# A two-layer hybrid decoder in fp32 parts: order of the first weights, place of the first norm's column and sums, and the last scale cut in parts

## The chip, the cores and the metric

The kernel runs on one core of a Trainium2 chip. The metric is device time in microseconds of one execution, as the median of several runs. The engines are called PE (TensorE, with PEld for its weight loads), DVE (VectorE), ACT (ScalarE), POOL (GpSimd) and SP (SyncE, which here only issues transfers). A name with q behind it (SPq, ACTq) is that engine's queue of instructions where it issues a DMA.

## The reference

A trunk of two layers over 256 tokens of width 1024. Each layer is a half-step SwiGLU (width 2816), attention, and a second half-step SwiGLU, each behind an RMS norm of the stream; a last RMS norm ends the trunk. Everything is float32.

```python
def rmsnorm(x, g):
    y = x * rsqrt(mean(x * x, axis=-1, keepdims=True) + RMS_EPS)
    return y * g

def swiglu(h, w_gate, w_up, w_down):
    return (silu(h @ w_gate) * (h @ w_up)) @ w_down

for layer in range(2):
    h = h + 0.5 * swiglu(rmsnorm(h, ffn1_norm[layer]), ...)
    hn = rmsnorm(h, mix_norm[layer])
    h = h + (mixer_a(hn, ...) if layer == 0 else mixer_b(hn, ..., shared))
    h = h + 0.5 * swiglu(rmsnorm(h, ffn2_norm[layer]), ...)
    if layer == 0:
        shared = shared_kv(h, kv_norm, kv_w, pos)
return rmsnorm(h, final_norm)
```

`mixer_a` is a causal dilated sliding-window attention with 16 heads of 64, `mixer_b` a block-sparse attention over shared keys and values. The change touches neither: it touches the first `swiglu` and the last `rmsnorm`.

## The kernel before

**Number format.** Each weight comes from memory as float32 (`raw`), and is cut in two parts in TensorE's reduced float format: ACT makes the high part `wh` by a copy (line 167, in the opening line 182), DVE the low part `wl` as the difference (line 168, in the opening line 183). Activations are cut in the same way. A product is then wh by (xh, xl), 512 columns wide (line 204), plus wl by xh, 256 wide (line 210). Where such a product adds in one PSUM bank, the first half of the bank and the second have to be summed at the end: `joined` (ACT copies one half at line 341, DVE adds the other at line 342).

**The feed-forward blocks.** `ffn_blocks` runs over the hidden width in 22 groups of 128 columns, f = 0 to 21. Weights come in units of two groups: one transfer of 1 MB for gate (g) and one for up (u), each split in two halves. Their order on SP's queue is the order of the calls. The pool of raw tiles has 4 buffers, that of wh and wl 8 each. Accumulators come from a pool of 5 PSUM banks (`accp`) and another of 3 (`trp`); a group needs one for gate and one for up. `close` sums and scales a finished group, and makes of it the operand of the down projection. It runs after the products of the next group have been issued.

**The opening.** For f = 0 and 1 of the first feed-forward block the weights come in five pieces over the contraction blocks k (`OPENING`: k = 0, k = 1, then two at a time), so that products can begin as soon as k = 0 is there. The x block of a piece (`first`, line 822; the first one carries the gains too) is transferred and scaled by the norm's gain (ACT line 99, DVE line 97) ahead of the piece's split. The gate weights of the first three pieces are issued on ACT's queue (line 113), everything else on SP's queue. Eight products of PE on a constant tile (line 119) run meanwhile.

**The norm.** The products use x times its gain only; the factor 1/rms belongs to the token and is put on the finished group. `Norm.square` sums the squares of the blocks (ACT line 245, DVE line 246 for the first norm). `Norm.finish` makes the column of 1/rms: a product on PE (line 251), its reader on DVE (line 253), a power on POOL (line 255). `Norm.spread` makes a row of it, the same on all partitions: two diagonal matrices on DVE (line 262), two products on PE (line 263), a copy on DVE (line 265). `close` multiplies by that row (line 372 on DVE, line 375 on POOL), so `spread` runs ahead of the first `close`. For the first block `finish` is called by `products_t` between the first products of gate and up at f = 2.

**The end.** `down_last` closes the four quarters of the last down projection (two token tiles t, two column halves c). Each close is followed by DVE's sum into h (line 590; line 595 for the last 256 columns), ACT's sum of squares (line 886; DVE line 882 for the last 256) and DVE's product with the final gain (line 890). `total` and the power (lines 894 and 902) run on POOL. `finish` then scales the 1024 columns of the token tile, half on ACT (line 903) and half on DVE (line 904), and sends the two halves (line 906).

**Order on an engine.** A scheduler orders the instructions of each engine from the order in the code and its own model of durations; `issue_after`, used through `queued` and `marks`, holds an instruction back in that order until a named one has been placed. Each engine then works through its list strictly in order.

Of the kernel before, what the change touches and what calls it, by code (L numbers as in the profile page):

```python
# [10 lines left out]
F32 = mybir.dt.float32  # L11
F32R = mybir.dt.float32r
AF = mybir.ActivationFunctionType
ALU = mybir.AluOpType

P = 128
S = 256
NT = S // P
D = 1024
KD = D // P  # L20
# [15 lines left out]
         ("ffn1_norm", 1), ("mix_norm", 1), ("ffn2_norm", 1)]  # L36

LAST_O = ("o", H // 2 - 1)
OPENING = ((0, 1), (1, 1), (2, 2), (4, 2), (6, 2))
GX = len(GAINS) * KD  # L40

# [26 lines left out]
def trunk(ctx: ExitStack, tc: tile.TileContext, a: dict, out: bass.AP):  # L68
    nc = tc.nc
    PS = bass.MemoryType.PSUM  # L70
    const = ctx.enter_context(tc.tile_pool(name="const", bufs=1))
    rawp = ctx.enter_context(tc.tile_pool(name="rawp", bufs=4))
# [35 lines left out]

    both = const.tile([P, GX + KD * S], F32, name="gains_hT")
    gT, hT = both[:, :GX], both[:, GX:].rearrange("p (k s) -> p k s", s=S)  # L110
    early = {k: rawp.tile([P, 2, n, S], F32, tag="raw", name=f"raw_0_{k}") for k, n in OPENING[:3]}
    for k, n in OPENING[:3]:
        nc.scalar.dma_start(early[k][:, 0], a["ffn1_w_gate"][0][k * P:(k + n) * P, :S].rearrange("(k p) n -> p k n", p=P))
    BF16 = mybir.dt.bfloat16
    fill = const.tile([P, 512], BF16, name="fill")
    nc.vector.memset(fill, 1.0)
# [37 lines left out]
    def unit(name, k, n, srcs, behind=()):  # L154

        raw = rawp.tile([P, k, n], F32, tag="raw", name=f"raw_{name}")
        for dst, src in srcs:
            nc.sync.dma_start(raw if dst is None else raw[:, :, dst], src)
        pieces = []
        behind = iter(behind)  # L160
        for j in range(0, k, 1024 // n):
            kk = min(1024 // n, k - j)
            wh = wp.tile([P, kk, n], F32R, tag="wh", name=f"wh_{name}_{j}")
            wl = wp.tile([P, kk, n], F32R, tag="wl", name=f"wl_{name}_{j}")
            r = raw[:, j:j + kk, :]
            with queued(next(behind, None)):
                nc.scalar.activation(wh, r, AF.Copy)  # L167
                nc.vector.tensor_sub(wl, r, wh.bitcast(F32))  # L168
            for i in range(kk):
                pieces.append((wh[:, i, :], wl[:, i, :]))  # L170
        return pieces

    def opening(wg, wu, before):


        for k, n in OPENING:
            raw = early.get(k) or rawp.tile([P, 2, n, S], F32, tag="raw", name=f"raw_0_{k}")
            wh, wl = [wp.tile([P, 2, n, S], F32R, tag=tag, name=f"{tag}_0_{k}") for tag in ("wh", "wl")]
            before(k, n)
            for i, w in list(enumerate((wg, wu)))[k in early:]:  # L180
                nc.sync.dma_start(raw[:, i], rows(w, k, n, 0, S))
            marks["opening"] = [nc.scalar.activation(wh, raw, AF.Copy)]
            nc.vector.tensor_sub(wl, raw, wh.bitcast(F32))
            for j in range(n):
                yield [(wh[:, i, j, :], wl[:, i, j, :]) for i in range(2)]

    def rows(w, k0, k, c0, n):
        return w[k0 * P:(k0 + k) * P, c0:c0 + n].rearrange("(k p) n -> p k n", p=P)
# [10 lines left out]
    def products_t(acs, wss, xs, first, last, between=None):  # L199


        for ac, ws in zip(acs, wss):
            for i, ((wh, wl), x) in enumerate(zip(ws, xs)):
                nc.tensor.matmul(ac, wh, flat(x), start=first and i == 0, stop=False)  # L204
            if between is not None:
                between()
                between = None
        for ac, ws in zip(acs, wss):
            for i, ((wh, wl), x) in enumerate(zip(ws, xs)):
                nc.tensor.matmul(ac[:, :S], wl, x[:, 0, :], start=False, stop=last and i == len(ws) - 1)  # L210
# [127 lines left out]
    def joined(ac, name):  # L338

        s = etile(f"j_{name}")  # L340
        nc.scalar.activation(s, ac[:, S:], AF.Copy)  # L341
        nc.vector.tensor_add(s, ac[:, :S], s)  # L342
        return s
# [13 lines left out]
    def ffn_blocks(name, wg, wu, norm, first=None, beside=(), sums=None, queue=()):  # L357

        blocks, pairs, rest = [], {}, []

        def both(f, pair):
            acs = [acc(f"{name}_{n}{f}") for n in "gu"]
            cols = slice(f % 2 * P, (f % 2 + 1) * P)
            products_t(acs, [[(wh[:, cols], wl[:, cols]) for wh, wl in w] for w in pair], norm.x, True, True,
                       norm.finish if norm.col is None else None)
            return acs

        def close(f, gate, up):  # L370
            g = joined(gate, f"{name}_g{f}")
            nc.vector.tensor_mul(g, g, norm.row)  # L372
            nc.scalar.activation(g, g, AF.Silu)  # L373
            u = joined(up, f"{name}_u{f}")
            nc.gpsimd.tensor_tensor(u, u, norm.row, op=ALU.mult)  # L375
            pair = f // 2
            if sums is not None and pair in sums:
                if f % 2 == 0:
                    pairs[pair] = atile([P, 2, S], name=f"act2_{name}_{f}")
                prod = pairs[pair][:, f % 2]  # L380
            else:
                prod = g
            nc.vector.tensor_mul(prod, g, u)  # L383
            x = atile([P, 2, S], F32R, name=f"act_{name}_{f}")
            parts_of(x[:, 0], x[:, 1], prod)
            while rest:
                rest.pop(0)()
            if prod is not g and f % 2:
                rest.extend(quarter_sums(pairs.pop(pair), *sums[pair], f"{name}_{f}"))
            blocks.append(x)  # L390

        done = []

        def close_all():
            if done and norm.row is None:
                norm.spread()
            for args in done:
                close(*args)
            done.clear()

        for f in range(0, KF, 2):
            if f == 0 and first is not None:
                ws = opening(wg, wu, first)
            else:
                ws = zip(*[unit(f"{name}_{n}{f}", KD, S, [(None, rows(w, 0, KD, f * P, S))], queue[2 * f + j:2 * f + j + 2])
                           for n, w, j in (("g", wg, 0), ("u", wu, 2))])
            if f == 0:
                acs = [[(trt if i and n == "u" else acc)(f"{name}_{n}{i}") for n in "gu"] for i in range(2)]
                for k, pair in enumerate(ws):
                    for i in range(2):  # L410
                        for ac, (wh, wl) in zip(acs[i], pair):
                            cols = slice(i * P, (i + 1) * P)
                            products_t([ac], [[(wh[:, cols], wl[:, cols])]], norm.x[k:k + 1], k == 0, k == KD - 1)
                    while norm.late:
                        norm.late.pop(0)()
                if first is not None:
                    with queued("opening"):
                        for k in range(KD):
                            norm.square(k)
                elif norm.col is None:  # L420
                    norm.finish()
                done += [(i, *acs[i]) for i in range(2)]
                continue
            pair = list(zip(*ws))
            for call in beside[f // 2 - 1:f // 2]:
                call()
            for i in (f, f + 1):
                acs = both(i, pair)
                close_all()
                done.append((i, *acs))  # L430
        close_all()
        return blocks

# [14 lines left out]
    def ffn(name, layer, which, norm, after, first=None, beside=(), homes=("kx4", "kx6", "qkh", "qkh"), queue=()):  # L448
        wg, wu, wd = (a[f"ffn{which}_w_{n}"][layer] for n in ("gate", "up", "down"))
        sums = left_sums(homes)  # L450
        blocks = ffn_blocks(name, wg, wu, norm, first, beside, sums, queue)
        if which == 1:
            table(AF.Exp, blocks[-1][:, 0, 0:1].bitcast(F32))
        down(f"{name}_d", wd, blocks, sums, after)
# [371 lines left out]
    n0, n1, n2 = Norm(0, "n0", nc.vector), Norm(1, "n1"), Norm(2, "n2")  # L826
    n3, n5, n6 = Norm(4, "n3"), Norm(5, "n5"), Norm(6, "n6")

    ffn("f10", 0, 1, n0, n1, first)
    late_constants()  # L830
    xs = n1.xs()
    w, n = a["a_w_qkv"][0], HG * DH
# [66 lines left out]
    def finish(t):  # L899
        v = total(t) if len(parts[t]) > 1 else parts[t][0]  # L900
        r = sp.tile([P, 1], F32, tag="rmsf", name=f"rms_{t}")
        nc.gpsimd.tensor_tensor(r, v, expo, op=ALU.pow)
        nc.scalar.activation(outs[t][0], outs[t][0], AF.Copy, scale=r)
        nc.vector.tensor_scalar_mul(outs[t][1], outs[t][1], r)
        for c in range(2):
            (nc.scalar, nc.sync)[c].dma_start(out[0, t * P:(t + 1) * P, c * 512:(c + 1) * 512], outs[t][c])

    down_last("f21_d", a["ffn2_w_down"][1], blocks, sums, h, 0.5, finish_part, finish)

# [26 lines left out]
```

## Time and profile before

| | us |
|---|---|
| median of the 3 runs | 979.35 |
| lowest and highest of them | 978.72, 980.27 |
| profiled execution | 978.82 |
| its span, first to last instruction | 977.0 |
| busy: PE, PEld, DVE, ACT, POOL | 966.6, 832.2, 813.9, 612.2, 286.0 |

A row of the order of time has the start in us, the duration in us (from the first start to the last end where it stands for several), the engine, the line, the operation with what it writes and reads, the shapes, the count, and in brackets how long the engine was idle before it and what ended that. A row of the chain of waits has the start, the duration, and the engine and line that the end of the span hung on for that time; "issue" is time in which the engine waited for nothing that the profile shows. Names in rows are those of the tiles without their numbers: `raw` is a piece of the opening, `raw_f_g` and `raw_f_u` are units of gate and up, `gains_hT` the x blocks. Ends of matrix products are modelled, since they are pipelined.

### The profile page before, as it was taken

How to read it: one execution, taken by the hardware profiler on the slowest of the kernel's cores; microseconds unless marked ns; L12 is line 12 of the kernel's file. 1: busy time of each engine (PE TensorE's matmuls, PEld its weight loads, DVE VectorE, ACT ScalarE, POOL GpSimd, SP SyncE). 2: the span in 40 equal slices, each digit the busy share in tenths (PEclk: the TensorE clock that was granted, in tenths of full speed). 3: DMA queues.
4: the chain of work that ended last, by engine and by line, in shares of the span. 5: the costliest groups of instructions: out<-in, count | busy, mean ns of one | idle time of the engine just before them, and what ended most of it. 6: DMA issues, size and time to landing. Idle time of an engine off the chain costs nothing.

```text
span 977.0 us, 14859 instructions
## 1 busy us (share of the span) xinstructions
PE 966.6 (99%) x5391; PEld 832.2 (85%) x5391; DVE 813.9 (83%) x1390; ACT 612.2 (63%) x1131; POOL 286.0 (29%) x235
## 2 busy tenths in 40 slices
PE   9999999999999999999999999999999999999997
PEld 6888888878889888888888888888888998888886
DVE  7988899887878788889898888987787878888995
ACT  7756656566777665656576655656577766666561
POOL 0211246143432211146032121612143322112461
PEclk9999999999999999999999999999999999999999
DMA  9876536664334656545755565483734345665351
GB/s 314 285 218 202 185 129 229 206 212 163 122 104 148 189 181 195 184 158 199 256 172 174 173 181 208 169 278 114 256 127 133 108 154 171 186 201 175 130 172 43
DMA packets 126858, 176.00 MB, mean 180 GB/s; under 512 B 3393, under 2 KB 106305, under 8 KB 126785
## 3 DMA queue, kind: packets, MB, share of 16 engines
q1 hardware_dynamic: 125936, 174.01, 54.9%
q10 hardware_dynamic: 848, 1.05, 0.3%
q8 instruction: 42, 0.69, 0.3%
q14 instruction: 32, 0.25, 0.1%
HBM read 173.99 MB, written 1.05 MB: 179 GB/s over the span
## 4 chain that ended last, share of the span: by engine, by line
PE 93%; DVE 2%; DMA 2%; ACT 2%; issue 1%; POOL 0%; SPq 0%; POOLq 0%; ACTq 0%; DVEq 0%
PE f_g L204 16%; PE f_u L204 16%; PE f_u L210 8%; PE f_g L210 8%; PE dn_f_d L197 6%; PE dn_f_d L193 6%; PE dn_f_d L195 6%; PE dn_f_d_m L197 1%; PE dn_f_d_m L193 1%; PE dn_f_d_m L195 1%; PE qk_a L193 1%; PE qk_a L197 1%; PE qk_a L195 1%; DMA raw_f_u<-in_ffn_w_up_dram 1%; PE v_a L193 1%; PE q_b L193 1%
## 5 line engine op out<-in xcount | busy, mean ns | idle before, releaser
L375 POOL TENSOR_TENSOR j_f_u<-j_f_u,r_n 128x256 f32<-128x256 f32 x88 | 93.7, 1067 | 355.9 <-DVE j_f_u L342 339.6
L204 PE MATMUL f_g<-x_n,wh_f_g 128*128 128x512 f32 x688 | 180.4, 394 | 1.0 <-DVE j_f_g L342 1.0
L204 PE MATMUL f_u<-x_n,wh_f_u 128*128 128x512 f32 x688 | 177.3, 390 | 0.0
L204 PEld LDWEIGHTS f_u<-x_n,wh_f_u 128*128 128x128 f32 x688 | 129.1, 188 | 27.3
L204 PEld LDWEIGHTS f_g<-x_n,wh_f_g 128*128 128x128 f32 x688 | 124.0, 189 | 23.9 <-DVE j_f_g L342 1.2
L168 DVE TENSOR_TENSOR wl_f_u<-raw_f_u,wh_f_u 128x1024 fp32r<-128x1024 f32 x86 | 113.0, 1317 | 1.0 <-ACT wh_f_u L167 1.0
L168 DVE TENSOR_TENSOR wl_f_g<-raw_f_g,wh_f_g 128x1024 fp32r<-128x1024 f32 x86 | 104.9, 1236 | 0.8 <-ACT wh_f_g L167 0.7
L210 PE MATMUL f_u<-x_n,wl_f_u 128*128 128x256 f32 x688 | 103.3, 283 | 0.0
L210 PE MATMUL f_g<-x_n,wl_f_g 128*128 128x256 f32 x688 | 102.9, 282 | 0.0
L210 PEld LDWEIGHTS f_g<-x_n,wl_f_g 128*128 128x128 f32 x688 | 96.4, 190 | 6.3
L167 ACT ACTIVATE wh_f_u<-raw_f_u 128x1024 fp32r<-128x1024 f32 x86 | 88.0, 1048 | 11.8 <-PE f_g L204 7.5
L167 ACT ACTIVATE wh_f_g<-raw_f_g 128x1024 fp32r<-128x1024 f32 x86 | 89.4, 1048 | 5.1 <-PE f_g L204 2.7
L373 ACT ACTIVATE j_f_g<-j_f_g 128x256 f32<-128x256 f32 x88 | 36.7, 417 | 88.5 <-DVE j_f_g L372 88.2
L210 PEld LDWEIGHTS f_u<-x_n,wl_f_u 128*128 128x128 f32 x688 | 91.6, 192 | 0.0
L246 POOL TENSOR_TENSOR ss_n<-ss_n,sq_n 128x256 f32<-128x256 f32 x35 | 32.2, 921 | 141.2 <-ACT sq_n L245 139.4
L99 ACT ACTIVATE act_f<-j_f_g 128x256 fp32r<-128x256 f32 x58 | 24.0, 418 | 55.3 <-DVE j_f_g L383 55.3
L383 DVE TENSOR_TENSOR j_f_g<-j_f_g,j_f_u 128x256 f32<-128x256 f32 x58 | 27.4, 477 | 29.9 <-POOL j_f_u L375 29.9
L492 POOL TENSOR_TENSOR sum_f_d_6b<-sum_f_d_6ac,raw_f_d 128x512 f32<-128x512 f32 x4 | 44.4, 11092 | 17.6 <-DVE sum_f_d_6ac L491 13.2
L342 DVE TENSOR_TENSOR j_f_g<-f_g,j_f_g 128x256 f32<-128x256 f32 x88 | 36.6, 416 | 11.8 <-ACT j_f_g L341 11.8
L685 POOL TENSOR_SCALAR sm_a<-sm_a,ls_a 128x128 f32<-128x128 f32 (+1 forms) x32 | 30.4, 964 | 47.8 <-DVE ls_a L683 42.1
L685 POOL TENSOR_SCALAR sm_b<-sm_b,ls_b 128x128 f32<-128x128 f32 (+1 forms) x32 | 29.0, 924 | 49.9 <-DVE ls_b L683 45.9
L372 DVE TENSOR_TENSOR j_f_g<-j_f_g,r_n 128x256 f32<-128x256 f32 x88 | 40.5, 463 | 0.7
(566 smaller groups left out, 2378.2 us busy)
## 6 DMA issues: line engine op xcount, KB each, us to landing
raw_f_d<-in_ffn_w_down_dram SPq DMA_DIRECT2D x44, 1024.0 KB, 5.0
raw_f_g<-in_ffn_w_gate_dram SPq DMA_DIRECT2D x43, 1024.0 KB, 5.4
raw_f_u<-in_ffn_w_up_dram SPq DMA_DIRECT2D x43, 1024.0 KB, 5.4
raw_qka<-in_a_w_qkv_dram SPq DMA_DIRECT2D x16, 512.0 KB, 4.7
raw_va<-in_a_w_qkv_dram SPq DMA_DIRECT2D x4, 1024.0 KB, 6.3
raw_ao<-in_a_w_o_dram SPq DMA_DIRECT2D x4, 1024.0 KB, 4.9
raw_kvb<-in_kv_w_dram SPq DMA_DIRECT2D x8, 512.0 KB, 4.1
raw_qb<-in_b_w_q_dram SPq DMA_DIRECT2D x4, 1024.0 KB, 5.2
```

The lines of the kernel that those rows point to most:

```text
L167: nc.scalar.activation(wh, r, AF.Copy)
L168: nc.vector.tensor_sub(wl, r, wh.bitcast(F32))
L193: nc.tensor.matmul(ac, xh, wh, start=first, stop=False)
L195: nc.tensor.matmul(ac, xh, wl, start=False, stop=False)
L197: nc.tensor.matmul(ac, xl, wh, start=False, stop=last)
L204: nc.tensor.matmul(ac, wh, flat(x), start=first and i == 0, stop=False)
L210: nc.tensor.matmul(ac[:, :S], wl, x[:, 0, :], start=False, stop=last and i == len(ws) - 1)
L372: nc.vector.tensor_mul(g, g, norm.row)
L373: nc.scalar.activation(g, g, AF.Silu)
L375: nc.gpsimd.tensor_tensor(u, u, norm.row, op=ALU.mult)
L492: nc.gpsimd.tensor_tensor(b[:, 0], ac[:, 0], raw[:, 3], op=ALU.add)
L685: nc.gpsimd.tensor_scalar(sm[:, seg], sm[:, seg], ls[:, t:t + 1], None, op0=ALU.mult)
```

## The change

Three things are changed.

First, the transfers of the opening. ACT's queue carries the gate weights of piece 0, the up weights of piece 0 and the up weights of piece 1 (`EARLY`), where it carried the gate weights of pieces 0, 1 and 2. The gate weights of pieces 1 and 2 are on SP's queue, behind the x block of their piece.

Second, the first norm and the first sums. At f = 2 only the gate weights are split before `products_t` is called. The up weights' unit is made within the call, behind `norm.finish`, and its splits are held behind the column's reader (`queue` names "n0" for them). In the first feed-forward block the two sums (`joined`) of group 0 are issued ahead of `spread`, where they were part of `close` behind it.

Third, `finish` at the end. For each token tile ACT scales 384 columns where it scaled 512, and DVE scales 256, 128 and 256 in three instructions where it scaled 512 in one. The 1024 columns are sent in three transfers (256 columns on SP's queue, 512 on ACT's, 256 on SP's), where there were two of 512.

In the instruction lists the number of DVE's instructions goes up by four and of SP's by two. On PE, within the opening two products of the fifth contraction block go behind another; at f = 2 five of gate's second products stand ahead of up's first products, where it was one, and one product of f = 3 stands among up's second products. On DVE and ACT the order differs up to the splits of f = 8, and then again only in the last scale. On SP the transfers of `rot`, `masks` and `gfin` stand together behind the up unit of f = 8, where there were units between them.

```diff
+EARLY = ((0, 0), (0, 1), (1, 1))
 OPENING = ((0, 1), (1, 1), (2, 2), (4, 2), (6, 2))
...
-    early = {k: rawp.tile([P, 2, n, S], F32, tag="raw", name=f"raw_0_{k}") for k, n in OPENING[:3]}
-    for k, n in OPENING[:3]:
-        nc.scalar.dma_start(early[k][:, 0], a["ffn1_w_gate"][0][k * P:(k + n) * P, :S].rearrange("(k p) n -> p k n", p=P))
+    early = {k: rawp.tile([P, 2, n, S], F32, tag="raw", name=f"raw_0_{k}") for k, n in OPENING[:2]}
+    for k, i in EARLY:
+        w = a["ffn1_w_up" if i else "ffn1_w_gate"][0]
+        nc.scalar.dma_start(early[k][:, i], w[k * P:(k + 1) * P, :S].rearrange("(k p) n -> p k n", p=P))
...
-            for i, w in list(enumerate((wg, wu)))[k in early:]:
-                nc.sync.dma_start(raw[:, i], rows(w, k, n, 0, S))
+            for i, w in enumerate((wg, wu)):
+                if (k, i) not in EARLY:
+                    nc.sync.dma_start(raw[:, i], rows(w, k, n, 0, S))
...
+        def weights(f, n):
+            j = 2 * f + 2 * (n == "u")
+            return unit(f"{name}_{n}{f}", KD, S, [(None, rows(wu if n == "u" else wg, 0, KD, f * P, S))], queue[j:j + 2])
...
-            products_t(acs, [[(wh[:, cols], wl[:, cols]) for wh, wl in w] for w in pair], norm.x, True, True,
-                       norm.finish if norm.col is None else None)
+            wss = [[(wh[:, cols], wl[:, cols]) for wh, wl in w] for w in pair]
+
+            def column():
+                norm.finish()
+                if len(pair) == 1:
+                    pair.append(weights(f, "u"))
+                    wss.append([(wh[:, cols], wl[:, cols]) for wh, wl in pair[1]])
+
+            products_t(acs, wss, norm.x, True, True, column if norm.col is None else None)
...
-        def close(f, gate, up):
-            g = joined(gate, f"{name}_g{f}")
+        def close(f, gate, up, g=None, u=None):
+            g = joined(gate, f"{name}_g{f}") if g is None else g
             nc.vector.tensor_mul(g, g, norm.row)
             nc.scalar.activation(g, g, AF.Silu)
-            u = joined(up, f"{name}_u{f}")
+            u = joined(up, f"{name}_u{f}") if u is None else u
...
             if done and norm.row is None:
+                if first is not None:
+                    f, *acs = done[0]
+                    done[0] += tuple(joined(ac, f"{name}_{n}{f}") for n, ac in zip("gu", acs))
                 norm.spread()
...
-    ffn("f10", 0, 1, n0, n1, first)
+    ffn("f10", 0, 1, n0, n1, first, queue=(None,) * 6 + ("n0",) * 2)
...
-        nc.scalar.activation(outs[t][0], outs[t][0], AF.Copy, scale=r)
-        nc.vector.tensor_scalar_mul(outs[t][1], outs[t][1], r)
-        for c in range(2):
-            (nc.scalar, nc.sync)[c].dma_start(out[0, t * P:(t + 1) * P, c * 512:(c + 1) * 512], outs[t][c])
+        first, own, rest, left = outs[t][1][:, :S], outs[t][0][:, :384], outs[t][1][:, S:], outs[t][0][:, 384:]
+        nc.scalar.activation(own, own, AF.Copy, scale=r)
+        for part in (first, left, rest):
+            nc.vector.tensor_scalar_mul(part, part, r)
+        for engine, part, c0 in ((nc.sync, first, 512), (nc.scalar, outs[t][0], 0), (nc.sync, rest, 512 + S)):
+            engine.dma_start(out[0, t * P:(t + 1) * P, c0:c0 + part.shape[-1]], part)
```

More of the change, by code (lines that the diff above doesn't have):

```diff
@@ L404, in ffn_blocks @@
             else:
-                ws = zip(*[unit(f"{name}_{n}{f}", KD, S, [(None, rows(w, 0, KD, f * P, S))], queue[2 * f + j:2 * f + j + 2])
-                           for n, w, j in (("g", wg, 0), ("u", wu, 2))])
+                ws = [weights(f, n) for n in ("g" if norm.col is None and f else "gu")]
             if f == 0:
+                ws = ws if first is not None else zip(*ws)
                 acs = [[(trt if i and n == "u" else acc)(f"{name}_{n}{i}") for n in "gu"] for i in range(2)]
@@ L423, in ffn_blocks @@
                 continue
-            pair = list(zip(*ws))
+            pair = ws
             for call in beside[f // 2 - 1:f // 2]:
```

## The prediction

> **What bounds the kernel now.** I read the page first, then the busy time by stretches, then both ends of the span in order of time, with the chain of waits there. The page:
>
> ```profile
> span 977.0 us, 14859 instructions
> ...
> PE 93%; DVE 2%; DMA 2%; ACT 2%; issue 1%; POOL 0%; SPq 0%; POOLq 0%; ACTq 0%; DVEq 0%
> ```
>
> TensorE (PE) is 93% of the chain that ended last: a change pays only where PE stands waiting, ahead of its first product, or behind its last. The profiled execution took 978.82 us, 1.82 more than its span; the median of the runs, 979.35, is 0.53 above it. The sum is made against 978.82, and 0.53 is added at the end.
>
> **Part 1, the order of the first weights.** The stretches (busy time of PE, PEld, DVE, ACT, POOL, then the granted clock, the DMA share, GB/s):
>
> ```profile
> 4.00:8.00 4.00, 3.32 (x12) 2.13 (x11) 1.98 (x4) 2.15 (x5) 0.00 (x0) 1.00 1.00 342
> 8.00:12.00 4.00, 3.93 (x20) 2.60 (x19) 3.58 (x7) 3.80 (x8) 0.00 (x0) 1.00 1.02 325
> ```
>
> The transfers are saturated at 325 to 342 GB/s (share 1.00 and above). What PE and its suppliers wait for there, in order of time, and one link of the chain and one row of the DMA issues (count, size, median us to landing):
>
> ```profile
> 3.61 0.38 SPq L181 DMA_DIRECT2D raw<-in_ffn_w_up_dram  x1
> ...
> 7.02 0.63 ACT L182 ACTIVATE wh<-raw 128x512 fp32r<-128x512 f32 x1 [1.05 <-DMA raw<-in_ffn_w_up_dram]
> ...
> 7.65 0.91 ACT L99 ACTIVATE x_n<-gains_hT 128x256 fp32r<-128x256 f32 x2
> ...
> 7.70 0.50 PE L204 MATMUL f_g<-x_n,wh 128*128 128x512 f32 x1 [0.68 <-ACT wh L182]
> ...
> 8.02 0.47 SPq L181 DMA_DIRECT2D raw<-in_ffn_w_up_dram  x1
> ...
> 8.46 1.04 ACT L182 ACTIVATE wh<-raw 128x1024 fp32r<-128x1024 f32 x1
> ...
> 9.56 0.50 PE L204 MATMUL f_g<-x_n,wh 128*128 128x512 f32 x1
> ...
> 12.58 1.06 ACT L182 ACTIVATE wh<-raw 128x1024 fp32r<-128x1024 f32 x1 [0.21 <-DMA raw<-in_ffn_w_up_dram]
> ...
> 12.81 0.40 PE L204 MATMUL f_g<-x_n,wh 128*128 128x512 f32 x1
> ```
>
> ```profile
> 5.02 5.40 DMA raw<-in_ffn_w_up_dram
> ```
>
> ```profile
> raw<-in_ffn_w_up_dram SPq DMA_DIRECT2D x3, 256.0 KB, 4.7
> ```
>
> The second block's split waited for its up weights until 7.02, and PE began that block at 7.70. When did the third block's up weights land, issued at 3.61? Of the three 256 KB up transfers one took 5.40 and one, issued at 8.02, had landed by 12.58, so took under 4.6; the median of 4.7 is then the first one's: it landed at 8.31. Its split began at 8.46, when ACT was through with the x blocks.
>
> Before, ACT's queue carries gate 0, gate 1 and the 256 KB of gate 2; after, gate 0, up 0 and up 1, and gate 2 follows on SP's queue behind the third x block. Ahead of the second block's last byte lay 156 + 5 x 128 + 256 = 1052 KB (the tiles' sizes in the code), after 796 KB: 256 KB less, 0.75 us at the rate above, so this block can begin some 0.75 us sooner. But the third block needs the same 1564 KB in both orders, and with the transfers saturated its last byte comes at 8.31 again. Only the 0.15 us by which ACT was late (8.46) goes, less a semaphore: **-0.12 us**. What the second block wins PE stands out before the third, at 9.44 instead of 9.56. Later blocks don't bind: the fourth one's data are there at 5.02 + 5.40 = 10.42 and PE reaches it at 12.81. Bounds: if the bytes do come sooner, the third split could begin when ACT has done wh_1 (7.65, less 0.75) and the x blocks (0.91 with overlap 0.81): 7.7, so -0.75. If the gate 2 transfer costs SP's queue one issue more ahead of up 2 (0.38, the row at 3.61), +0.4. I take the saturated case, to which the stretches are nearest.
>
> The Trainium skill (DMA: Bandwidth & Descriptors, "Issuing engines are not separate DMA queues") speaks against a gain here: transfers begun by ScalarE and SyncE run on the same 16 DMA engines and interleave, and a second issuer saves issue time alone. The share of 1.00 agrees. By that rule this part gives -0.12; by a queue with a speed of its own, -0.75.
>
> **Part 2, norm's column and the first sums.** Groups f = 2 and f = 3 of the hidden columns, up to the start of f = 4 and f = 5:
>
> ```profile
> 18.36 2.01 PE L204 MATMUL f_g<-x_n,wh_f_g 128*128 128x512 f32 x8
> ...
> 19.30 2.01 ACT L167 ACTIVATE wh_f_u<-raw_f_u 128x1024 fp32r<-128x1024 f32 x2 [1.00 <-DMA raw_f_u<-in_ffn_w_up_dram]
> ...
> 20.21 0.50 PE L251 MATMUL col_n<-mean,ss_n 128*128 128x1 f32 x4
> ...
> 20.40 2.35 DVE L168 TENSOR_TENSOR wl_f_u<-raw_f_u,wh_f_u 128x1024 fp32r<-128x1024 f32 x2
> ...
> 20.58 0.36 PE L210 MATMUL f_g<-x_n,wl_f_g 128*128 128x256 f32 x1
> ...
> 22.67 0.15 DVE L253 TENSOR_SCALAR v_n<-col_n 128x2 f32<-128x2 f32 x1
> ...
> 23.46 1.11 PE L210 MATMUL f_u<-x_n,wl_f_u 128*128 128x256 f32 x8
> ...
> 23.66 0.48 DVE L262 TENSOR_SCALAR diag_n<-ident,c_n 128x128 f32<-128x128 f32 x2 [0.83 <-POOL c_n L255]
> ...
> 24.42 0.60 PE L263 MATMUL row_n<-diag_n,ones 128*128 128x128 f32 x4
> ...
> 25.52 0.41 DVE L342 TENSOR_TENSOR j_f_g<-f_g,j_f_g 128x256 f32<-128x256 f32 x1
> ...
> 25.99 2.11 PE L204 MATMUL f_g<-x_n,wh_f_g 128*128 128x512 f32 x8 [0.97 <-DVE j_f_g L342]
> ```
>
> ```profile
> 31.68 2.00 PE L204 MATMUL f_g<-x_n,wh_f_g 128*128 128x512 f32 x8
> ```
>
> ```profile
> 37.24 2.00 PE L204 MATMUL f_g<-x_n,wh_f_g 128*128 128x512 f32 x8
> ```
>
> PE makes norm's column at 20.21. Its reader on DVE (line 253) is queued behind both f_u splits (20.40, 2.35 long) and runs at 22.67; POOL's power, the diagonals (23.66), another split and the row's copy follow, and only at 25.52 the first sum j_f_g, which frees the accumulator that f = 3 needs. PE waits 0.97 us for it. From 18.36 to 31.68 are 13.32 us. Two groups take 2 x (37.24 - 31.68) = 11.12, the column 20.58 - 20.21 = 0.37, the row 0.60. The other 1.23 us are this wait and the restart behind it.
>
> After, DVE's order is: reader, first j_f_g sum, the two f_u splits, the j_f_u sum, two diagonals, next split, the row's copy. ACT does the two copies for these sums ahead of its f_u splits, in time that it has: those wait for data until 19.30, of a transfer that isn't moved (SP issues it in the same place). The queue past which things are moved is DVE's: behind the reader now stand the f_u splits, and PE's second f_u products wait for them.
>
> In times: reader some 0.1 us behind the column's 20.21 + 0.50, at 20.8; sum to 21.2 (0.41), so the accumulator is free 3 us before PE asks; f_u splits 21.1 to 23.5, 0.7 later than before; j_f_u to 23.8; diagonals to 24.2; the row's copy about 25.3, as before. PE's order changes too: five second products of f_g go ahead of f_u, one product of f = 3 into f_u's second products. Eight first products take 1.85 (18.36 to 20.21), eight second ones 0.96 (23.46 to 24.42). So PE needs the last f_u split at 18.36 + 1.85 + 0.37 + 0.60 + 1.85 + 0.36 + 0.48 + 0.23 = 24.1 and the diagonals at 24.6, or 0.12 sooner with part 1: in time by 0.5 and 0.3 us. The 1.23 goes: **-1.2 us**. Next late is nothing that I find up to f = 5: f = 4's bank comes free with the next sums, near 26, against a start near 30.4. Bounds: -1.35 with part 1's lead used in full; -0.6 if the diagonals are late by as much as they now are early and the restart stays.
>
> The small constants go out together behind up 8, where their first users are stages away: nothing. If their 0.9 MB push the next weights back, that is 2.7 us of transfer at 340 GB/s, against weights that are loaded a pair of groups (11.1 us) ahead of PE.
>
> **Part 3, the last scale in parts.** In order of time, then the chain, then the issues:
>
> ```profile
> 968.30 0.68 DVE L590 SCALAR_TENSOR_TENSOR h<-dn_f_d,h 128x512 f32<-128x512 f32 x1
> ...
> 972.72 0.72 ACT L903 ACTIVATE out<-out,rms 128x512 f32<-128x512 f32 x1 [1.87 <-POOL rms L902]
> 972.73 0.48 DVE L904 TENSOR_SCALAR out<-out,rms 128x512 f32<-128x512 f32 x1 [0.47 <-POOL rms L902]
> 973.48 0.35 ACTq L906 DMA_DIRECT2D out_dram<-out  x1
> ```
>
> ```profile
> 967.89 0.49 DVE out L904
> 968.38 0.61 DVE h L590
> ...
> 969.01 0.69 DVE out L890
> 969.71 0.61 DVE h L590
> ...
> 970.34 0.52 ACT sq L886 x2
> ...
> 970.95 0.31 POOL var L894
> ```
>
> ```profile
> out_dram<-out SPq DMA_DIRECT2D x2, 256.0 KB, 2.1
> out_dram<-out ACTq DMA_DIRECT2D x2, 256.0 KB, 2.5
> ```
>
> DVE's scale of 512 columns is a step of 0.41 (967.89 to 968.30), 0.08 under its duration; the two diagonals of 128 columns take 0.48 together (23.66), so 0.20 a step; 256 lie between, 0.27. Three parts of 256, 128 and 256 take 0.74.
>
> On the last token tile: first part done after 0.35 instead of 0.48, third after 0.82. ACT scales 384 columns instead of 512; its copies take 1.04 for 1024 and 0.63 for 512 columns, 0.8 ns each, so its 256 KB leave 0.10 sooner, at 973.38. The third part leaves at 973.58 with 128 KB. All bytes are as before, and the first leave 0.13 sooner: **-0.15 us**. Bounds: the last transfer lands 2.1 after 973.58, where ACT's landed 2.5 after 973.48: -0.3; it takes 2.5 from the end of its issue (0.35 later): +0.45.
>
> But the first token tile is scaled in the same three parts, and there DVE is in the chain: at 967.89 it holds up the sum of the next tile (968.30), and each step from there to 970.95 follows the last within 0.1 us. 0.74 in place of 0.41: **+0.33 us**, in full. The part's net is +0.18, between 0 and +0.8.
>
> **Sum:** -0.12 - 1.2 + 0.18 = -1.14. 978.82 - 1.14 + 0.53 = **978.2 us**. Between the two ends every engine's order is as it was, so the lead is carried through.
>
> **Rivals.**
> 1. The third block's bytes do come sooner (-0.75): 977.6, and 977.3 with part 3 at its good end, 977.2 with part 2 at its own too. For it: ACT's queue is empty sooner. Against: the share of 1.00. Chance 0.32.
> 2. Slower: the reader holds DVE. How soon it can run behind PE's column isn't shown, for it was queued until 22.67. If it runs then again, with the f_u splits behind it, these end at 25.4, the diagonals at 26.1, the row at 26.7, and PE, which has the row ahead of all but one of f = 3's products, resumes 0.7 later than its 25.99: 978.82 + 0.7 - 0.12 + 0.18 + 0.53 = 980.1. It decides from a reader later than 22.0. Against: the column has ended at 20.71. Chance 0.07.
> 3. The lead is given back where a later stage waits for transfers, and only the tail is left, 978.82 + 0.18 + 0.53 = 979.5. Against: DMA is 2% of the chain. Chance 0.11.
>
> **Numbers.** Forecast 0.50; rivals 0.32, 0.07, 0.11. The runs scatter by some 0.8 us about their median. 0.2%, about what a measurement of this kernel can tell from no change, is 1.96 us: under 977.4 is faster, over 981.3 slower. Of rival 1 0.6 lies under it (0.19), of the forecast 0.22 by scatter and its better ends (0.11): faster 0.30. Over 981.3 lies only what of rivals 2 and 3 meets scatter and a tail of +0.8: slower 0.05. Same 0.65. The range goes from rival 1's best, 977.2 less some scatter, 976.9, to 979.5 of rival 3.
>
> **What would show it.** Right: the 0.97 before f = 3 gone and f = 4 beginning near 30.4; the second block beginning near 7.0 and the third not before 9.4; DVE's first scale 0.74 long and POOL's last power 0.33 later against the last product. Wrong: the third block at 8.8, a wait of PE at the row, or a lead at 31 us that has shrunk at 960.

## The result

The changed kernel takes 977.35 us (median; 976.85 to 978.16), the kernel before 979.26 us in the same comparison. The ratio is 0.9981, with a 95% interval of 0.9973 to 0.9989: faster by 1.9 us, between 1.1 and 2.6, just short of the 0.2% (1.96 us) at which the prediction drew its line for faster. The forecast was 978.2 within 976.9 to 979.5. The profiled execution of the changed kernel took 977.35 us with a span of 975.6, against 978.82 and 977.0 before.

The page after. PE's share of the chain rose by a point:

```profile
PE 94%; DVE 2%; ACT 2%; DMA 1%; issue 1%; POOL 0%; POOLq 0%; DVEq 0%; ACTq 0%
```

The opening in order of time: ACT's splits of the second and third piece of weights and PE's first products of these pieces.

```profile
3.60 0.38 SPq L184 DMA_DIRECT2D raw<-in_ffn_w_up_dram  x1
...
6.42 0.63 ACT L185 ACTIVATE wh<-raw 128x512 fp32r<-128x512 f32 x1 [1.07 <-DMA raw<-in_ffn_w_up_dram]
...
7.10 0.49 PE L207 MATMUL f_g<-x_n,wh 128*128 128x512 f32 x1 [0.18 <-ACT wh L185]
...
8.11 1.06 ACT L185 ACTIVATE wh<-raw 128x1024 fp32r<-128x1024 f32 x1 [0.26 <-DMA raw<-in_ffn_w_up_dram]
...
9.22 0.50 PE L207 MATMUL f_g<-x_n,wh 128*128 128x512 f32 x1 [0.20 <-ACT wh L185]
```

The second piece's split begins at 6.42 instead of 7.02, and PE takes that piece up at 7.10 instead of 7.70. The third one's split now waits for its data and begins at 8.11 instead of 8.46, PE at 9.22 instead of 9.56: a lead of 0.34.

The groups f = 2 and f = 3:

```profile
18.05 2.01 PE L207 MATMUL f_g<-x_n,wh_f_g 128*128 128x512 f32 x8
...
19.90 0.50 PE L254 MATMUL col_n<-mean,ss_n 128*128 128x1 f32 x4
...
20.46 0.15 DVE L256 TENSOR_SCALAR v_n<-col_n 128x2 f32<-128x2 f32 x1
20.53 0.41 DVE L345 TENSOR_TENSOR j_f_g<-f_g,j_f_g 128x256 f32<-128x256 f32 x1
...
20.86 2.35 DVE L170 TENSOR_TENSOR wl_f_u<-raw_f_u,wh_f_u 128x1024 fp32r<-128x1024 f32 x2
...
23.46 0.47 DVE L265 TENSOR_SCALAR diag_n<-ident,c_n 128x128 f32<-128x128 f32 x2
...
24.33 0.61 PE L266 MATMUL row_n<-diag_n,ones 128*128 128x128 f32 x4
...
24.70 1.86 PE L207 MATMUL f_g<-x_n,wh_f_g 128*128 128x512 f32 x7
...
30.13 2.00 PE L207 MATMUL f_g<-x_n,wh_f_g 128*128 128x512 f32 x8
```

The column's reader runs at 20.46 where it ran at 22.67, the first sum at 20.53 where it ran at 25.52, and the f_u splits behind them at 20.86 instead of 20.40. PE makes the row and goes on with f = 3 without a wait. From f = 2 to f = 4 it takes 30.13 - 18.05 = 12.08 us where it took 13.32.

The end:

```profile
966.42 0.81 DVE L923 TENSOR_SCALAR out<-out,rms 128x256 f32<-128x256 f32 x3 [1.13 <-POOL rms L919]
...
967.15 0.68 DVE L607 SCALAR_TENSOR_TENSOR h<-dn_f_d,h 128x512 f32<-128x512 f32 x1
...
969.07 0.28 PE L200 MATMUL dn_f_d_end<-wh_f_d_10b,act_f 128*128 128x256 f32 x1
...
970.13 0.48 DVE L899 CUSTOM_DVE_ANT_0 sq<-h,var 128x256 f32<-128x256 f32 x1 [0.18 <-POOL var L911]
...
971.43 0.81 DVE L923 TENSOR_SCALAR out<-out,rms 128x256 f32<-128x256 f32 x3 [0.46 <-POOL rms L919]
```

The first tile's three parts hold DVE until the next sum at 967.15, 0.73 behind their start; one part held it 0.41. The last scale begins 2.36 us behind the start of PE's last product (971.43 - 969.07), where it was 2.19 (972.73 - 970.54). From there to the span's end are 4.17 us, where 4.27 were.

So the span's 1.40 us are: opening -0.31 (f = 2 at 18.05 instead of 18.36), the groups -1.24, the whole middle from f = 4 to the last product +0.08 (938.94 against 938.86), the way to the last scale +0.17, the rest -0.10.

### The profile page after: what moved, and what is told of

Read it like the earlier page. It is cut to its first block, busy times and chain, and to the rows that moved or that the text cites. A ratio compares the mean times of both kernels' runs of the same rounds, so it can differ in the third digit from the quotient of the medians.

```text
span 975.6 us, 14863 instructions
## 1 busy us (share of the span) xinstructions
PE 966.4 (99%) x5391; PEld 831.9 (85%) x5391; DVE 813.5 (83%) x1394; ACT 611.5 (63%) x1131; POOL 284.9 (29%) x235
## 4 chain that ended last, share of the span: by engine, by line
PE 94%; DVE 2%; ACT 2%; DMA 1%; issue 1%; POOL 0%; POOLq 0%; DVEq 0%; ACTq 0%
PE f_g L207 17%; PE f_u L207 16%; PE f_u L213 9%; PE f_g L213 9%; PE dn_f_d L200 6%; PE dn_f_d L196 6%; PE dn_f_d L198 6%; PE dn_f_d_m L200 1%; PE dn_f_d_m L196 1%; PE dn_f_d_m L198 1%; PE qk_a L196 1%; PE qk_a L200 1%; PE qk_a L198 1%; PE v_a L196 1%; PE q_b L196 1%; PE kv_b L196 1%
```

## The experiments

Theory at the start: three parts with separate effects as in this list, the largest one from the place of the first sums. Rivals: the parts need each other; the queue of the first weights has a speed of its own; only the place of the column's reader counts.

**Part 1 alone**, the first two changes of the diff (`EARLY`, and the loop in `opening`) on the kernel before:

```diff
-    for k, n in OPENING[:3]:
-        nc.scalar.dma_start(early[k][:, 0], a["ffn1_w_gate"][0]...)
+    for k, i in EARLY:
+        nc.scalar.dma_start(early[k][:, i], w[...]...)
```

> Part 1 alone, on the kernel before: the first weights' order. Theory A (the transfers are saturated, so only what ACT was late goes, and the third block's bytes come a little sooner as the changed kernel's trace shows, 8.09 instead of 8.31): the third block starts at 9.2 on PE instead of 9.56, f = 2 at 18.05 instead of 18.36, and the wait before f = 3 stays at about 1.0 us; the time is 0.3 us under before. Rival B (a queue of its own has a speed of its own): the third block at 8.8, 0.75 us under before. Rival C (the opening's lead is lost at the wait before f = 3, because that wait ends by DVE's clock and not by PE's): f = 3 starts at 25.99 as before with a longer wait, and the time is that of before.

978.48 us, ratio 0.9993 (0.9984 to 1.0002): the gain can't be told from none by the measured time. Its order of time:

```profile
18.22 2.01 PE L207 MATMUL f_g<-x_n,wh_f_g 128*128 128x512 f32 x8
...
20.61 0.16 DVE L256 TENSOR_SCALAR v_n<-col_n 128x2 f32<-128x2 f32 x1
...
24.91 0.42 DVE L268 COPY r_n<-row_n 128x256 f32<-128x256 f32 x1 [0.34 <-PE row_n L266]
...
25.72 2.14 PE L207 MATMUL f_g<-x_n,wh_f_g 128*128 128x512 f32 x8 [0.85 <-DVE j_f_g L345]
```

The scheduler here put the column's reader at 20.61, ahead of the f_u splits, although part 2 isn't in. PE still waits 0.85 us before f = 3. So the reader's late place in the kernel before isn't all that made the wait: here DVE stood idle for 0.34 us until PE's row product was there, and the sum came behind the row's copy. The time, 0.4 us under the 978.9 of the kernel before in this comparison, is near A's 0.3 but not clear of none; A's starts came 0.2 later than it said. B falls with the third piece on PE at 9.39. C is not settled: f = 3 came 0.27 sooner than in the profile before, but the reader's place had changed too, and the other executions of the kernel before and of part 3 alone have f = 3 anywhere from 25.61 to 26.07.

**Part 2 alone**, the changes in `ffn_blocks` and the `queue` of the first call on the kernel before:

> Part 2 alone, on the kernel before: norm's column and first sums ahead. Theory A: f = 2 starts at 18.36 as before, the column's reader runs near 20.75, the wait of 0.97 before f = 3 is gone, f = 4 starts at 30.45 instead of 31.68, and the time is 1.2 us under before. Rival B (the gain needs part 1's order, or the splits now late make PE wait): PE waits before the row or within f_u's second products, f = 4 starts after 30.9, and the time is at most 0.7 us under before.

977.76 us, ratio 0.9985 (0.9976 to 0.9994).

```profile
18.60 2.01 PE L204 MATMUL f_g<-x_n,wh_f_g 128*128 128x512 f32 x8
...
24.77 0.60 PE L263 MATMUL row_n<-diag_n,ones 128*128 128x128 f32 x4
...
25.13 2.09 PE L204 MATMUL f_g<-x_n,wh_f_g 128*128 128x512 f32 x8
...
30.80 2.00 PE L204 MATMUL f_g<-x_n,wh_f_g 128*128 128x512 f32 x8
```

The wait is gone here too: 30.80 - 18.60 = 12.20 us for the two groups. Theory A holds, and nearly its size (1.1 us under the 978.9 of the kernel before); f = 2 began 0.24 later than in the kernel before, since the second piece of weights landed later with the same transfers (its split at 7.40 instead of 7.02), so f = 4 is at 30.80 and not at 30.45.

**Part 3 alone**, `finish` of the diff on the kernel before:

> Part 3 alone, on the kernel before: both token tiles scaled in parts. Theory A: DVE's sum for the second tile starts 0.32 later against the first tile's scale, the last power starts 0.17 later against the last product (the last sum's own wait for PE hid the rest), and the span's end behind that power is 0.10 nearer: 0.07 us over before. Rival B (the cut scale pays): the end is 0.2 us nearer to the last product than before. Opening and middle as before in both.

979.2 us, ratio 0.9999 (0.999 to 1.0008).

```profile
970.30 0.28 PE L197 MATMUL dn_f_d_end<-wh_f_d_10b,act_f 128*128 128x256 f32 x1
...
972.67 0.81 DVE L906 TENSOR_SCALAR out<-out,rms 128x256 f32<-128x256 f32 x3 [0.46 <-POOL rms L902]
```

The last scale begins 2.37 behind the last product's start, and the span, 976.8, ends 4.13 behind that: +0.18 and -0.14 against 2.19 and 4.27. In the trace theory A holds: the cut scale gives with one hand what it takes with the other. The measured time can't tell 0.07 more from 0.2 less.

**The last tile alone in parts**, on the changed kernel:

```diff
+        if t == 0:
+            nc.scalar.activation(outs[t][0], outs[t][0], AF.Copy, scale=r)
+            nc.vector.tensor_scalar_mul(outs[t][1], outs[t][1], r)
+            ...
+            return
         first, own, rest, left = ...
```

> The changed kernel with the first token tile scaled as before (one instruction of 512 columns on DVE and two transfers) and the last one in parts. Theory A (the first tile's three instructions stand on the chain): the last power is back to 1.47 us behind the last product's start instead of 1.64, the parts of the last tile still bring 0.10, so the end is 0.17 us nearer than in the changed kernel, 0.10 nearer than before. Rival B (the last power waits for PE's last product anyway): no difference from the changed kernel. The time is that of the changed kernel within what can be measured in both.

977.33 us, ratio 0.998 (0.9971 to 0.9989), the changed kernel's within what can be told.

```profile
969.22 0.28 PE L200 MATMUL dn_f_d_end<-wh_f_d_10b,act_f 128*128 128x256 f32 x1
...
971.40 0.81 DVE L929 TENSOR_SCALAR out<-out,rms 128x256 f32<-128x256 f32 x3 [0.47 <-POOL rms L919]
```

The last scale is back at 2.18 behind the last product's start, and the span, 975.6, ends 4.20 behind it, 0.07 nearer than the 4.27 before. So the delay of 0.17 came from the first tile's parts, as theory A has it.

**The column without the sums ahead**, on the changed kernel:

```diff
-                if first is not None:
-                    f, *acs = done[0]
-                    done[0] += tuple(joined(ac, f"{name}_{n}{f}") for n, ac in zip("gu", acs))
                 norm.spread()
```

> The changed kernel without the first sums ahead: group 0 is summed in its close again, behind the row. The column's reader stays ahead of the f_u splits. Theory A (the wait before f = 3 is for the accumulator that the first sum frees, and the reader's place matters only through it): reader near 20.46, f_u splits 20.5 to 22.9, diagonals near 23.0, next split to 24.2, row's copy after the row product at about 24.6, first sum done near 25.1; PE, which has the row behind all of f_u's second products, ends the row at 24.7 and waits 0.3 to 0.5 us there; f = 4 starts near 30.6, 0.5 later than in the changed kernel. Rival B (the reader's place alone makes the gain): f = 4 at 30.13.

978.47 us, ratio 0.9991 (0.9981 to 1.0).

```profile
17.82 2.01 PE L207 MATMUL f_g<-x_n,wh_f_g 128*128 128x512 f32 x8
...
20.26 0.15 DVE L256 TENSOR_SCALAR v_n<-col_n 128x2 f32<-128x2 f32 x1
...
23.86 0.60 PE L266 MATMUL row_n<-diag_n,ones 128*128 128x128 f32 x4
...
24.50 0.42 DVE L268 COPY r_n<-row_n 128x256 f32<-128x256 f32 x1 [0.29 <-PE row_n L266]
...
25.31 2.14 PE L207 MATMUL f_g<-x_n,wh_f_g 128*128 128x512 f32 x8 [0.85 <-DVE j_f_g L345]
...
31.02 2.00 PE L207 MATMUL f_g<-x_n,wh_f_g 128*128 128x512 f32 x8
```

With the reader at 20.26, PE waits 0.85 us all the same, more than the 0.3 to 0.5 expected, and the two groups take 13.20. The bracket of the row copy says why: DVE waited for PE's row product (23.86 + 0.60). PE waits for a sum that is queued behind the copy of PE's own product: it stands through DVE's copy and sum each time, whatever comes before. The sums ahead of the row are worth 13.20 - 12.08 = 1.12 us: the 0.85 of the wait, and 0.27 behind it whose place isn't shown. The early reader alone is worth 0.1 to 0.3: with it the two groups take 13.20 here and 13.21 in part 1 alone, without it 13.32, 13.51 and 13.35 in the three executions of the kernel before and 13.53 in part 3 alone.

**The sums without the hold**, on the changed kernel: the up unit made before the products, no `queue`.

```diff
-                ws = [weights(f, n) for n in ("g" if norm.col is None and f else "gu")]
+                ws = [weights(f, n) for n in "gu"]
...
-    ffn("f10", 0, 1, n0, n1, first, queue=(None,) * 6 + ("n0",) * 2)
+    ffn("f10", 0, 1, n0, n1, first)
```

> The changed kernel with the up unit of f = 2 made before the products again and its splits not held behind the column's reader; the first sums stay ahead of the row. In the instruction lists DVE's order is the same as the changed kernel's all the same (reader, first sum, splits); on ACT the up splits can stand ahead of the first copies again. Theory A (the sums ahead are what counts, and they let the reader go forward): f = 4 starts within 0.2 us of 30.13 and the time is that of the changed kernel. Rival B (the hold counts): the wait before f = 3 is back by 0.5 us or more.

977.45 us, ratio 0.998 (0.9971 to 0.9989).

```profile
17.86 2.01 PE L207 MATMUL f_g<-x_n,wh_f_g 128*128 128x512 f32 x8
...
29.93 2.00 PE L207 MATMUL f_g<-x_n,wh_f_g 128*128 128x512 f32 x8
```

12.07 us for the two groups, as with the hold: it does nothing here that the order of the sums doesn't bring by itself.

**Gate 2 on ACT's queue**, on the changed kernel, so that the bytes are the same and the queue differs:

```diff
-EARLY = ((0, 0), (0, 1), (1, 1))
+EARLY = ((0, 0), (0, 1), (1, 1), (2, 0))
```

> The changed kernel with gate 2 (256 KB) as the fourth transfer of ACT's queue instead of SP's. The bytes ahead of the third block are the same. Theory A (bytes decide): the second block's split starts 0.2 to 0.5 later than the 6.42 of the changed kernel, since gate 2 shares the engines with its last transfers, the third block's up weights land at 8.1 to 8.3 and f = 2 starts within 0.2 us of 18.05. Rival B (two queues together carry more than one): the third block's data land 0.3 us or more sooner, PE starts it before 8.9. Rival C: the fourth issue on ACT pushes the table load and the first split back by 0.45 us, and the first product starts at 5.4 instead of 5.00 without any effect on f = 2.

978.27 us, ratio 0.999 (0.998 to 0.9999).

```profile
7.27 0.63 ACT L186 ACTIVATE wh<-raw 128x512 fp32r<-128x512 f32 x1 [1.82 <-DMA raw<-in_ffn_w_up_dram]
...
8.74 1.06 ACT L186 ACTIVATE wh<-raw 128x1024 fp32r<-128x1024 f32 x1
...
18.84 2.00 PE L208 MATMUL f_g<-x_n,wh_f_g 128*128 128x512 f32 x8
...
21.16 0.61 PE L255 MATMUL col_n<-mean,ss_n 128*128 128x1 f32 x4 [0.32 <-DVE ss_n L250]
```

The second piece's split begins at 7.27, the third one's at 8.74, f = 2 at 18.84. The third piece's up weights landed at 8.72, 0.4 us later than in any execution of the changed order, and f = 2 came 0.56 later, against A's "within 0.2" and B's "sooner"; C falls, for the first product began at 5.17, as in two executions of the changed order. But this doesn't show that the queue decides: the kernel before has gate 2 on ACT's queue too, and there the same piece lands between 7.57 and 8.49 (below). The time doesn't part the two either, for more than the queue changed: the scheduler put a sum of squares behind the first sum on DVE, the column's product waits 0.32 for it, and the two groups take 12.65 us (f = 4 at 31.49) where they took 12.08. And the profiled execution, 978.82, is the second slowest of the ten.

**256 KB more** ahead of gate 2, on the changed kernel (data that nobody uses):

```diff
+            if k == 2:
+                nc.sync.dma_start(gfin[:, :2 * S].rearrange("p (k n) -> p k n", n=S), rows(a["ffn1_w_up"][1], 0, 2, 0, S))
```

> The changed kernel with one more transfer of 256 KB on SP's queue ahead of gate 2, of data that nobody uses (into a tile that is loaded properly later). Theory A (the transfers are saturated, bytes decide): the third block's up weights land 0.75 us later, near 8.85, all later blocks of the opening too, PE starts the third block near 9.95 and f = 2 0.6 to 0.75 later than 18.05 as far as PE has no slack behind it; the time is 0.6 us over the changed kernel. Rival B (landing is set by the issue, 4.5 us behind it, not by the bytes): landing moves by one issue time at most, 0.45, and f = 2 by less than 0.3.

978.41 us, ratio 0.9987 (0.9978 to 0.9997).

```profile
4.13 0.47 SPq L186 DMA_DIRECT2D raw<-in_ffn_w_up_dram  x1
...
8.44 1.06 ACT L187 ACTIVATE wh<-raw 128x1024 fp32r<-128x1024 f32 x1 [1.07 <-DMA raw<-in_ffn_w_up_dram]
...
18.41 2.01 PE L209 MATMUL f_g<-x_n,wh_f_g 128*128 128x512 f32 x8
```

The up weights of the third piece are issued at 4.13 instead of 3.60, they land at 8.35, their split begins at 8.44 and f = 2 at 18.41. Against the means of the changed order below, the split (8.07) and f = 2 (18.03) are 0.4 later: half of A's 0.75, and more than B's bound of 0.3 for f = 2, though only 0.1 outside the scatter. But the profiled execution, 977.80, is the fastest of the ten; by the ratios to the kernel before, 0.9987 against the changed kernel's 0.9981, the cost is 0.6 us, as A says, with intervals that overlap. So A's size is neither shown nor refuted, and since the issue moved too, the run doesn't part bytes and issue.

**The two kernels again**, for the scatter of the opening.

> The kernel before, unchanged, profiled once more, to learn how far the opening differs between executions of one program. So far the third block's split began at 8.46, 8.73 and 7.74 with the order of weights before, at 8.11, 8.28, 8.21, 7.90 and 7.84 with the changed order. Theory A (part 1 brings some 0.2 us, under a scatter of 0.4): a start between 7.7 and 8.8, f = 2 between 17.8 and 18.6. Rival B (8.46 and 18.36 are fixed and the third kernel was an exception): within 0.1 of these. From f = 2 to f = 4 it takes 13.2 to 13.5 us in both.

> The kernel before once more, for the same question: third block's split between 7.7 and 8.8 by theory A, 8.46 by rival B.

> The changed kernel, profiled once more. Theory A: the third block's split begins between 7.8 and 8.4, f = 2 between 17.8 and 18.3, f = 2 to f = 4 takes 12.07 as in the profile at hand. Rival B: 8.11 and 18.05 again within 0.1.

In that order:

```profile
8.28 1.05 ACT L182 ACTIVATE wh<-raw 128x1024 fp32r<-128x1024 f32 x1
...
18.28 2.04 PE L204 MATMUL f_g<-x_n,wh_f_g 128*128 128x512 f32 x8
```

```profile
8.15 1.04 ACT L182 ACTIVATE wh<-raw 128x1024 fp32r<-128x1024 f32 x1
...
18.24 1.99 PE L204 MATMUL f_g<-x_n,wh_f_g 128*128 128x512 f32 x8
```

```profile
8.33 1.06 ACT L185 ACTIVATE wh<-raw 128x1024 fp32r<-128x1024 f32 x1 [0.50 <-DMA raw<-in_ffn_w_up_dram]
...
18.28 2.01 PE L207 MATMUL f_g<-x_n,wh_f_g 128*128 128x512 f32 x8
...
30.36 2.00 PE L207 MATMUL f_g<-x_n,wh_f_g 128*128 128x512 f32 x8
```

978.99, 978.83 and 977.59 us. With all profiled executions of an order together:

| | second split | third split | f = 2 | executions |
|---|---|---|---|---|
| weights ordered as before | 6.25 to 7.40, mean 6.87 | 7.74 to 8.73, mean 8.27 | 17.80 to 18.60, mean 18.26 | 5 |
| changed order | 5.80 to 6.42, mean 6.11 | 7.82 to 8.33, mean 8.07 | 17.80 to 18.28, mean 18.03 | 7 |

The orders are those of the weights: the first line has the kernel before and parts 2 and 3 alone, the second the changed kernel, part 1 alone and the runs that change only other things. The second piece comes 0.76 us sooner, with ranges that hardly overlap; f = 2 some 0.2 sooner, within a scatter of 0.8. Theory A holds in size, not as a proof, and rival B falls: 8.28, 8.15 and 8.33 are not within 0.1 of 8.46 and 8.11.

The start of a split is not the landing of its data. The profile gives the time from issue to landing, and by it the third piece's up weights land at 7.57 to 8.49, mean 8.08, with the order before, and at 7.80 to 8.31, mean 8.05, with the changed one: they came no sooner. With the order before the split begins 0.12 to 0.25 behind that landing, mean 0.19, for ACT is still at the x blocks; with the changed order it begins 0.02 behind it each time.

The groups scatter less: the changed kernel takes 30.36 - 18.28 = 12.08 again.

**Combined**: the last tile alone in parts, and no hold (both edits above).

> The changed kernel with the first token tile scaled as before and without the hold on the up splits of f = 2 (what the runs point to). Theory: f = 2 to f = 4 in 12.07, the last scale begins 2.18 behind the start of PE's last product and the span ends 4.1 to 4.2 behind that, so 0.17 us under the changed kernel, less than the runs can tell; ratio to the kernel before 0.997 to 0.999.

977.38 us, ratio 0.9984 (0.9974 to 0.9993): no better than the changed kernel by the measured time.

```profile
17.80 2.04 PE L207 MATMUL f_g<-x_n,wh_f_g 128*128 128x512 f32 x8
...
29.90 2.00 PE L207 MATMUL f_g<-x_n,wh_f_g 128*128 128x512 f32 x8
```

Its spans between marks are as expected: 12.10, 2.18, and 4.20 to the end at 975.3.

## Why the prediction was right, and where it wasn't

**Sum.** Forecast: -0.12 for the opening, -1.2 for the groups, +0.18 for the end, -1.14 in all. The trace: -0.31, -1.24, +0.07 and +0.08 in between, -1.40. The median moved by 1.9; three profiled executions of the kernel before (978.82, 978.83, 978.99) against two of the changed one (977.35, 977.59) differ by 1.4, which lies within the interval of 1.1 to 2.6. The 0.85 us between the forecast of 978.2 and the measured 977.35 have two parts. The sum was 0.33 short of the 1.47 between the two profiled executions. The other 0.53 is the term added at the end: the profiled execution of the kernel before lay under its median, that of the changed one is its median. What the slower executions of the kernel before do otherwise no trace shows, so 0.44 of the 1.9 stays unexplained. By the number alone the result lies at rival 1's 977.3 and not at the forecast; by the mechanism it doesn't, as the landing of the third piece says. The three parts measured alone give ratios of 0.9993, 0.9985 and 0.9999, in product 0.9977, near the whole's 0.9981: that the parts need each other is not seen.

**Part 1.** The step held: the second piece comes 0.75 us sooner (forecast) or 0.76 (the two means), PE stands most of that out before the third, and the third piece lands no sooner (8.05 against 8.08 in the mean). What goes is the time by which ACT was late behind that landing, 0.19 in the mean, forecast 0.12. That DMA issuers share the same engines, which the Trainium skill states (DMA: Bandwidth & Descriptors, "Issuing engines are not separate DMA queues"), agrees with the landing that did not move. The reason given, that the bytes ahead decide when the third piece lands, is borne out by the equal means alone: neither run made to test it, with gate 2 on the other queue and with 256 KB more, settles it. What makes the landing differ by 0.9 us between executions with the same transfers stays open. The 0.31 of the two profiles is partly scatter, for the means differ by 0.2. The sign that PE would not begin the third piece before 9.4 failed (9.22), by less than that scatter.

**Part 2.** The size was right, and the later reader, splits and diagonals were in time as worked out (f_u splits 20.86 to 23.21, diagonals at 23.46, row at 24.33, forecast 24.2 for the diagonals' end). The step that failed is the cause: the prediction let the wait begin at the reader queued behind the f_u splits. Two runs with an early reader and the sums behind the row (part 1 alone, and the column without the sums) still wait 0.85. Beneath the reader lay a loop: the next group's accumulator was freed by a sum queued behind the copy of a product that PE makes last. In the kernel before DVE's own chain from the reader ended last, but not by much:

```profile
25.19 0.42 DVE L265 COPY r_n<-row_n 128x256 f32<-128x256 f32 x1
```

The copy ran right behind a split, 0.17 us after PE's row product was done (24.42 + 0.60), so an earlier reader could win little, and the wait went from 0.97 to 0.85. The arithmetic came out because the change, as the prediction counts it, moves the first sum ahead as well; had it moved only the reader, to which the account of the wait points, 1.12 of the 1.24 us would have been missing. Rival 2 priced the reader for the same wrong reason; the reader ran 0.56 after the column's product began.

**Part 3.** The cut of the last tile brought 0.07 to 0.14 in the traces, forecast 0.15. The first tile's 0.33 was mis-sized: DVE's next sum was indeed 0.32 late (0.73 against 0.41), but the last power came only 0.17 later. The failed step is "in full". The order of time of the kernel before, at the last sum and the sum of squares behind it:

```profile
970.54 0.28 PE L197 MATMUL dn_f_d_end<-wh_f_d_10b,act_f 128*128 128x256 f32 x1
...
970.86 0.42 DVE L595 SCALAR_TENSOR_TENSOR h<-dn_f_d_end,h 128x256 f32<-128x256 f32 x1
...
971.43 0.48 DVE L882 CUSTOM_DVE_ANT_0 sq<-h,var 128x256 f32<-128x256 f32 x1
```

The last sum (line 595) ran right behind PE's last product (970.54 + 0.28), and the sum of squares (line 882) right behind that, though POOL's part of it was there at 971.26. So PE bound this step before. In the changed kernel POOL's part is done 0.31 later against that product's start (1.03 behind it, where it was 0.72), and now the sum of squares waits for it (970.13, its bracket names POOL): it begins 1.06 behind the product's start instead of 0.89. So 0.14 of the delay was hidden where the step before had waited for PE, and 0.17 came through.

**The lead** was carried: 0.08 of 1.55 was lost in 939 us. Rival 3 fell, and rival 1 with the landing of the third piece.

## What to carry to other kernels

When an engine waits for a buffer, look at what the instruction that frees it is queued behind: here a sum needed nothing but finished products, and stood behind a copy of the waiting engine's own last product; issuing it sooner was worth 1.12 us, most of the change. Look also at what lies just beneath the chain that ends last, for it sets what a repair of that chain can win: here 0.12 of 0.97. A sooner landing of one transfer was worth little here, for the next one did not land sooner. Cutting a last step in parts paid on the last tile alone, by 0.07 to 0.14 in the traces; on the earlier tile the extra instructions stood ahead of the next tile's work.

## What the runs showed of the hardware that was not expected

The landing of the opening's transfers differs between executions with the same transfers: the third piece's up weights landed between 7.57 and 8.49 us in five executions with the order before, and between 7.80 and 8.31 in seven with the changed one. Meanwhile the 12.07 to 12.10 us of the two groups behind them repeat to 0.03 in six executions of the kernels with the sums ahead and the changed order of weights (gate 2 on the other queue aside). And the choice of queue didn't visibly move that landing in the mean: with the same bytes ahead, 512 KB of them on ACT's queue in the order before and 384 KB in the changed one, it was 8.08 and 8.05.
